# Two output projections emitted at block 13 instead of block 8 of the second chunk's FFN, their first loads tied to that block by one-column copies

## The chip, the cores and the metric

The kernel runs on one core of one Trainium2 chip. The metric is the device time of one execution in microseconds; the time before is the median of three runs, 3060.2 us. TensorE (PE), VectorE (DVE), ScalarE (ACT) and GpSimd (POOL) each work through their own instructions in the order in which the program lists them. SyncE (SP) and ScalarE also issue DMA transfers, each from its own list.

## What is computed

One layer of a decoder trunk on 2048 tokens of width 1024, in float32. The reference, cut to what matters here:

```
p = rms_norm(x, norm1_g) @ w_in
mix = concat(mlstm(p), rwkv7(p), diff_attention(p))      # 256 + 256 + 512 columns
x = x + mix @ w_out                                      # the output projection
h = rms_norm(x, norm2_g)
x = x + square(relu(h @ w_ff_up)) @ w_ff_down            # the FFN, width 4096
out = rms_norm(x, final_g)
```

Attention is causal, has 4 heads and works on blocks of 128 queries.

## The kernel before

The tokens are cut into four chunks of 512, numbered 0 to 3. After the input projection and the two recurrent groups, attention runs chunk after chunk and head after head (class `Attention`, lines 1004 to 1071). For a block of 128 queries it multiplies Q with K into PSUM tiles `pS` (lines 1026, 1027, 1029), moves them to the row `E` on DVE (L1030), takes exponentials on ACT (L1037), combines two rows on DVE (L1045), transposes `E` on PE into `pT` (L1051), copies it to `PT` on ACT (L1053) and multiplies it with V into `pO` (L1056). After four blocks of a head the result is normalised, transposed (L1068), copied to the tile `ot` (L1070) and stored to the scratch tensor `mixT` (L1071).

The tail (class `Tail`) does the output projection and the FFN. Every matrix product is done in three matmuls, on high and low parts of both operands (lines 182, 183, 184). Weights come in quarters of 128x512: a load into `wraw`, a split on ACT into `whi` (L174) and on POOL into `wlo` (L175). `Weights.get` has six pairs of `whi` and `wlo`, and three `wraw` tiles, or two where it is made with `raws=2`.

`ffn(x, h)` runs 16 blocks for one chunk. `up(fb)` multiplies two slices of `w_ff_up` with the hidden tiles `hh`, `hl` into two `pd` tiles and makes `ah`, `al` from them; `down(fb)` multiplies these with a slice of `w_ff_down` into eight `py` tiles, each added to `x` on DVE (L1175). The generator yields after `up(fb)` and before `down(fb - 1)`. A block is 48 + 48 matmuls of 128x512.

Chunk 0's and chunk 1's FFN are done in this way, beside the attention of chunks 2 and 3. The projections of chunks 2 and 3 (`outproj(2, ...)`, `outproj(3, ...)`) need all of the attention; the FFN of these two chunks is done together at the end by the class `Wino`, with seven products in place of eight. `Wino.first` and `Wino.second` normalise the projected chunks; their sums are PSUM tiles `nps` out of the same pool `pd` of two tiles that `up` uses, and they stand in the program behind each projection.

What sets the order: a scheduler gives every instruction a place by priority, which is the order of emission in the Python code (`high_priority` puts some ahead), among those whose operands and tiles it holds to be ready. Tiles of one pool and tag are handed out in the order of emission, so a block of the FFN that is emitted behind `Wino.second` gets its `pd` tiles behind those of `Wino.second`, and so behind both projections. The code around the change:

```
for fb in tl.ffn(x1, h1):                       # chunk 1
    if fb == 0:
        tl.final(0, x0, (2, 5))
    if fb == 8:
        actx.close()                            # attention's pools end here
        ...                                     # pq, tx2, th2, tw2: new pools in their memory
        w2 = Weights(..., "tw2", raws=2)
        raw2 = lambda: w2.wp.tile([P, T], F32, name="xr", tag="xr", bufs=3)
        outproj(2, tl.load(2, hp2, raw2), ...); wn.first(x2)
        outproj(3, tl.load(3, hp2, raw2), ...); wn.second(x2, x3, hp2)
```

`tl.load(c)` loads eight tiles `xr` from `mixT` and splits them into `hh` and `hl` of the pool `th2`. The new pools lie in memory that attention used, so the first loads into `xr` and `wraw` wait until attention is done with it.

Of the kernel before, what the change touches and what calls it, by code (L numbers as in the profile page):

```python
# [10 lines left out]
F32 = mybir.dt.float32  # L11
# [9 lines left out]
P = 128  # L21
# [4 lines left out]
T = 512  # L26
# [146 lines left out]
def split(nc, hi, lo, src, lo_eng):  # L173
    nc.scalar.activation(hi, src, AF.Copy)  # L174
    lo_eng.tensor_tensor(lo, src, hi.bitcast(F32), ALU.subtract)  # L175


def mm3(nc, out, pairs):

    n = len(pairs)  # L180
    for i, (sh, sl, mh, ml) in enumerate(pairs):
        nc.tensor.matmul(out, sh, mh, start=(i == 0), stop=False)  # L182
        nc.tensor.matmul(out, sh, ml, start=False, stop=False)  # L183
        nc.tensor.matmul(out, sl, mh, start=False, stop=(i == n - 1))  # L184
# [890 lines left out]
class Tail:  # L1075
# [73 lines left out]
    def ffn(s, x2, h2):  # L1149
        tc, nc = s.tc, s.tc.nc  # L1150
        FB = 16
        acts = {}

        def up(fb):
            w = s.w.get(s.wu[fb], 256)
            ah = s.ap.tile([P, 2, T], F32R, name="ah", tag="ah")
            al = s.ap.tile([P, 2, T], F32R, name="al", tag="al")
            for j in range(2):
                ps = s.pd.tile([P, T], F32, name="pd", tag="pd")
                mm3(nc, ps, [(*w(k, j * P, (j + 1) * P), h2[k][0], h2[k][1]) for k in range(KT)])  # L1160
                with tc.high_priority():
                    r = s.raw()
                    nc.scalar.activation(r, ps, AF.Relu)
                    nc.scalar.activation(r, r, AF.Square)
                    split(nc, ah[:, j], al[:, j], r, nc.vector)
            acts[fb] = (ah, al)

        def down(fb):
            w = s.w.get(s.wd[fb], 1024, kt=2)
            ah, al = acts.pop(fb)  # L1170
            for d in range(KT):
                ps = s.py.tile([P, T], F32, name="py", tag="py")
                mm3(nc, ps, [(*w(j, d * P, (d + 1) * P), ah[:, j], al[:, j]) for j in range(2)])
                with tc.high_priority():
                    nc.vector.tensor_tensor(x2[d], ps, x2[d], ALU.add)  # L1175

        up(0)
        yield 0
        for fb in range(1, FB):
            up(fb)  # L1180
            yield fb
            down(fb - 1)
        yield FB
        down(FB - 1)
# [299 lines left out]
def tile_hybrid_layer(ctx: ExitStack, tc: tile.TileContext, xt, wi, wg, wm, wo, wu, wd, vf, vg, lw, hb, tb, lq, cm, out, dbg=None, upto=9):  # L1484
    nc = tc.nc
# [98 lines left out]
    tl = Tail(ctx, tc, e, xt, wo, wu, wd, out)  # L1584
# [12 lines left out]
    for fb in tl.ffn(x1, h1):  # L1597
        if fb == 0:
            tl.final(0, x0, (2, 5))
        if fb == 8:  # L1600
            actx.close()
            with tc.using_default_side("right"):
                pq = [ctx.enter_context(tc.tile_pool(name=f"pq{i}", bufs=2, space=PSUM)) for i in range(2)]
                tl.xp2 = ctx.enter_context(tc.tile_pool(name="tx2", bufs=1))
                hp2 = ctx.enter_context(tc.tile_pool(name="th2", bufs=8))
                w2 = Weights(tc, e, rctx.enter_context(tc.tile_pool(name="tw2", bufs=1)), raws=2)
            raw2 = lambda: w2.wp.tile([P, T], F32, name="xr", tag="xr", bufs=3)
            for _ in tl.outproj(2, tl.load(2, hp2, raw2), x2, (0, 1), w2, raw2, pq[0], e.x2d[0]):
                pass
            wn = Wino(tl, pq)  # L1610
            wn.first(x2)
            for _ in tl.outproj(3, tl.load(3, hp2, raw2), x3, (4, 5), w2, raw2, pq[1], e.x2d[1]):
                pass
            wn.second(x2, x3, hp2)
# [76 lines left out]
```

## Time and profile before

| | us |
|---|---|
| median of 3 runs (3052.37 to 3060.57) | 3060.2 |
| the profiled execution | 3062.33 |
| span of the profiled execution | 3060.6 |
| PE busy in the span | 2907.0 (95%) |
| DVE / ACT / POOL busy | 1936.0 / 1295.7 / 1063.1 |
| mean granted TensorE clock, share of full speed | 0.963 |

The profiled execution lies 2.1 us above the median and 1.7 us above its own span. PE is busy nearly all the time, but a busy share says little by itself: matmuls are pipelined, and at half the granted clock the same matmul counts as busy for longer. So the stretches in which PE pauses, or in which the granted clock is under 1.00, are the ones to look at; start times of matmuls that follow each other tell what one costs.

### The profile page before, as it was taken

How to read it: one execution, taken by the hardware profiler on the slowest of the kernel's cores; microseconds unless marked ns; L12 is line 12 of the kernel's file. 1: busy time of each engine (PE TensorE's matmuls, PEld its weight loads, DVE VectorE, ACT ScalarE, POOL GpSimd, SP SyncE). 2: the span in 40 equal slices, each digit the busy share in tenths (PEclk: the TensorE clock that was granted, in tenths of full speed). 3: DMA queues.
4: the chain of work that ended last, by engine and by line, in shares of the span. 5: the costliest groups of instructions: out<-in, count | busy, mean ns of one | idle time of the engine just before them, and what ended most of it. 6: DMA issues, size and time to landing. Idle time of an engine off the chain costs nothing.

```text
span 3060.6 us, 47580 instructions
## 1 busy us (share of the span) xinstructions
PE 2907.0 (95%) x16880; PEld 2383.8 (78%) x16880; DVE 1936.0 (63%) x4358; ACT 1295.7 (42%) x2567; POOL 1063.1 (35%) x1016
## 2 busy tenths in 40 slices
PE   8999999999999889999999999997799899999998
PEld 7887887778878767888888788875677688888886
DVE  6587878678772456554555765562435766668788
ACT  5333334223322445544445544552234355554443
POOL 4353444333433214433333423422345322222232
PEclk9998999999999879999999989997899899999999
DMA  8445333643543553444446343334522244475441
GB/s 308 129 135 196 92 92 84 214 118 92 154 147 115 165 143 107 111 121 112 113 109 171 96 122 104 105 88 134 172 85 85 69 168 152 149 255 179 146 147 63
DMA packets 317096, 409.15 MB, mean 134 GB/s; under 512 B 102421, under 2 KB 164150, under 8 KB 315834
## 3 DMA queue, kind: packets, MB, share of 16 engines
q1 hardware_dynamic: 230154, 285.90, 30.7%
q10 hardware_dynamic: 86704, 120.21, 13.3%
q8 instruction: 133, 2.18, 0.3%
q14 instruction: 105, 0.86, 0.1%
HBM read 298.24 MB, written 107.76 MB: 133 GB/s over the span
## 4 chain that ended last, share of the span: by engine, by line
PE 56%; DVE 5%; DMA 4%; ACT 1%; issue 1%; POOL 1%; SPq 0%; ACTq 0%; DVEq 0%; POOLq 0%
PE pd L183 5%; PE pd L182 5%; PE pd L184 5%; PE pd L1224 5%; PE pd L1225 5%; PE pd L1226 5%; PE pO L1056 4%; PE py L182 4%; PE py L183 4%; PE py L184 3%; PE pS L1026 2%; PE pS L1027 2%; PE pT L1051 2%; PE py L1226 2%; PE py L1224 2%; PE py L1225 2%
## 5 line engine op out<-in xcount | busy, mean ns | idle before, releaser
L175 POOL TENSOR_TENSOR wlo<-wraw,whi 128x512 fp32r<-128x512 f32 (+2 forms) x432 | 595.4, 1391 | 849.7 <-ACT whi L174 611.3
L174 ACT ACTIVATE whi<-wraw 128x512 fp32r<-128x512 f32 (+2 forms) x432 | 267.4, 624 | 334.6 <-PE pd L183 103.3
L182 PE MATMUL pd<-hh,whi 128*128 128x512 f32 x768 | 304.0, 402 | 18.6 <-ACT whi L174 9.7
L175 POOL TENSOR_TENSOR wlo<-wr,whi 128x512 fp32r<-128x512 f32 x104 | 151.2, 1455 | 462.6 <-ACT whi L174 356.0
L183 PE MATMUL pd<-hl,whi 128*128 128x512 f32 x768 | 305.2, 398 | 1.0 <-DVE hl L175 1.0
L184 PE MATMUL pd<-hh,wlo 128*128 128x512 f32 x768 | 300.4, 397 | 1.4 <-POOL wlo L175 1.4
L1175 DVE TENSOR_TENSOR x<-py,x 128x512 f32<-128x512 f32 x256 | 174.9, 688 | 196.0 <-PE py L184 195.4
L1030 DVE TENSOR_SCALAR_CACHE_REDUCE E<-pS 128x512 f32<-128x512 f32 (+4 forms) x320 | 186.0, 607 | 146.1 <-PE pS L1027 85.6
L174 ACT ACTIVATE whi<-wr 128x512 fp32r<-128x512 f32 x224 | 140.4, 630 | 244.6 <-PE pd L1225 163.6
L182 PE MATMUL pd<-hhi,whi 128*128 128x512 f32 x544 | 224.2, 416 | 8.3 <-ACT hhi L279 7.4
L184 PE MATMUL pd<-hhi,wlo 128*128 128x512 f32 x544 | 224.4, 415 | 0.0
L183 PE MATMUL pd<-hlo,whi 128*128 128x512 f32 x544 | 223.2, 412 | 0.4 <-POOL hlo L175 0.3
L1224 PE MATMUL pd<-hh,whi 128*128 128x512 f32 x560 | 221.0, 396 | 1.5 <-DVE x L1348 1.3
L1226 PE MATMUL pd<-hh,wlo 128*128 128x512 f32 x560 | 221.5, 396 | 0.0
L1225 PE MATMUL pd<-hl,whi 128*128 128x512 f32 x560 | 221.5, 396 | 0.0
L182 PE MATMUL py<-ah,whi 128*128 128x512 f32 x512 | 206.3, 403 | 10.0 <-DVE x L1175 5.0
L183 PE MATMUL py<-al,whi 128*128 128x512 f32 x512 | 203.3, 397 | 0.6 <-DVE al L175 0.6
L184 PE MATMUL py<-ah,wlo 128*128 128x512 f32 x512 | 202.4, 397 | 0.0
L1037 ACT ACTIVATE E<-E,nm 128x128 f32<-128x128 f32 (+15 forms) x128 | 153.7, 1201 | 95.5 <-DVE nm L1033 81.0
L182 PE MATMUL pd<-whi,hhi 128*128 128x256 f32 (+1 forms) x640 | 188.0, 294 | 2.6 <-ACT gates L372 1.5
L183 PE MATMUL pd<-wlo,hhi 128*128 128x256 f32 (+1 forms) x640 | 187.9, 294 | 0.0
L182 PEld LDWEIGHTS pd<-hh,whi 128*128 128x128 f32 x768 | 146.5, 192 | 52.6 <-issue 11.2
(453 smaller groups left out, 7021.3 us busy)
## 6 DMA issues: line engine op xcount, KB each, us to landing
act<-x SPq DMA_DIRECT2D x96, 256.0 KB, 2.1
wraw<-in_wu ACTq DMA_DIRECT2D x64, 256.0 KB, 3.1
wraw<-in_wu SPq DMA_DIRECT2D x64, 256.0 KB, 3.2
wraw<-in_wd ACTq DMA_DIRECT2D x64, 256.0 KB, 3.2
wraw<-in_wd SPq DMA_DIRECT2D x64, 256.0 KB, 3.1
x<-act SPq DMA_DIRECT2D x56, 256.0 KB, 2.7
x<-act ACTq DMA_DIRECT2D x56, 256.0 KB, 4.9
wraw<-in_wi ACTq DMA_DIRECT2D x48, 256.0 KB, 3.5
```

What stands on the lines that cost most here:

```text
L174: nc.scalar.activation(hi, src, AF.Copy)
L175: lo_eng.tensor_tensor(lo, src, hi.bitcast(F32), ALU.subtract)
L182: nc.tensor.matmul(out, sh, mh, start=(i == 0), stop=False)
L183: nc.tensor.matmul(out, sh, ml, start=False, stop=False)
L184: nc.tensor.matmul(out, sl, mh, start=False, stop=(i == n - 1))
L1030: V.tensor_scalar(E[:, k0:k0 + w], s_[:, :w], 0.125, None, ALU.mult, ALU.max, accum_out=mb[:, j:j + 1])
L1037: A.activation(E[:, :n], E[:, :n], AF.Exp, bias=nm, accum_out=l)
L1056: PE.matmul(o[:, 0:P], pt[:, b * P:(b + 1) * P], vt[:, kb], start=(kb == 0), stop=(kb == i))
L1175: nc.vector.tensor_tensor(x2[d], ps, x2[d], ALU.add)
L1224: mm(ps, sh, mv[0], start=start, stop=False, skip_group_check=True)
L1225: mm(ps, sh, mv[1], start=False, stop=False, skip_group_check=True)
L1226: mm(ps, sl, mv[0], start=False, stop=True, skip_group_check=True)
```

## The change

The two projections are emitted when the FFN of chunk 1 yields block 13, no longer at block 8. `up` leaves its last `ah` tile in `s.mark`. Ahead of the projections five tiles are taken, the three `xr` and the two `wraw` of the new pools, and ACT copies one column of `ah` of block 13 into each of them. A load into one of these tiles then has to come behind its copy, and a copy behind `up(13)` and behind attention's last use of that memory.

```diff
@@ ffn, up(fb)
             acts[fb] = (ah, al)
+            s.mark = ah
@@ tile_hybrid_layer
     for fb in tl.ffn(x1, h1):
-        if fb == 8:
+        if fb == 13:
             actx.close()
...
             raw2 = lambda: w2.wp.tile([P, T], F32, name="xr", tag="xr", bufs=3)
+
+            with tc.high_priority():
+                for t in [raw2() for _ in range(3)] + [w2.wp.tile([P, T], F32, name="wraw", tag="wraw", bufs=2) for _ in range(2)]:
+                    nc.scalar.copy(t[:, 0:1], tl.mark[:, 0, 0:1].bitcast(F32))
             for _ in tl.outproj(2, tl.load(2, hp2, raw2), x2, (0, 1), w2, raw2, pq[0], e.x2d[0]):
```

What this makes of the order is shown at three places. The first is PE at the end of attention (tile numbers kept: `py_23306` and `py_23314` are `down(11)`, `pd_23378` is the second half of `up(13)`; `pd_22632` and `pd_22662` are the first tiles of projection 2). Before:

```order
L1051 MATMUL pT_17328<-ident_63,E_17243 128x128 x4
L1056 MATMUL pO_17294<-Vt_16952,PT_17333 128x128 x4
L1068 MATMUL pT_17352<-ident_63,osb_16955 128x128 x4
L182 MATMUL pd_22632<-hh_22560,whi_22607 128x512
L182 MATMUL pd_22662<-hh_22560,whi_22607 128x512
```

With the change:

```order
L182 MATMUL py_23306<-ah_22998,whi_23253 128x512
L1068 MATMUL pT_17352<-ident_63,osb_16955 128x128 x2
L183 MATMUL py_23306<-al_22999,whi_23253 128x512
L1068 MATMUL pT_17352<-ident_63,osb_16955 128x128 x2
L184 MATMUL py_23306<-ah_22998,wlo_23254 128x512
L183 MATMUL pd_23378<-hl_20970,whi_23329 128x512
L184 MATMUL pd_23378<-hh_20969,wlo_23330 128x512
L182 MATMUL pd_23378<-hh_20975,whi_23329 128x512
L182 MATMUL py_23314<-ah_22998,whi_23241 128x512
```

Before, attention's last steps stand one behind the other and the projection right behind them; with the change the matmuls of blocks 9 to 13 stand between the steps, and 47 more of the FFN stand between attention's last transposes and the projection's first matmul.

The second place is SP's list at the same point (`wraw` from `in_wu`, `in_wd` are FFN weights, from `in_wo` projection weights). Before:

```order
L1071 DMA mixT_305<-ot 128x512 x2
L42 DMA xr<-mixT_304 128x512
L42 DMA wraw<-in_wo 128x512
L42 DMA xr<-mixT_304 128x512 x2
L42 DMA wraw<-in_wo 128x512
```

With the change:

```order
L42 DMA wraw<-in_wu 128x512 x2
L42 DMA wraw<-in_wd 128x512 x2
L1071 DMA mixT_305<-ot 128x512
L42 DMA xr<-mixT_304 128x512 x2
L42 DMA wraw<-in_wu 128x512
L42 DMA wraw<-in_wo 128x512
L42 DMA wraw<-in_wu 128x512
L42 DMA xr<-mixT_304 128x512 x2
L42 DMA wraw<-in_wd 128x512
```

Sixteen loads of FFN weights now stand between the last two stores to `mixT`, and three loads of FFN weights stand among the projection's first loads behind the last store.

The third place is ACT's list at the same point. Before:

```order
L1070 COPY ot<-pT 128x512
L42 DMA wraw<-in_wo 128x512
L42 DMA xr<-mixT_304 128x512
L174 ACTIVATE hh<-xr 128x512
L174 ACTIVATE whi<-wraw 128x512
```

With the change:

```order
L1070 COPY ot<-pT 128x512
L174 ACTIVATE whi<-wraw 128x512 x2
L174 ACTIVATE ah<-traw 128x512
L174 ACTIVATE whi<-wraw 128x512
L1612 COPY xr<-ah 128x1 x3
L42 DMA wraw<-in_wu 128x512
L1612 COPY wraw<-ah 128x1 x2
L42 DMA xr<-mixT_304 128x512
L42 DMA wraw<-in_wo 128x512
L1163 ACTIVATE traw<-pd 128x512
L174 ACTIVATE whi<-wraw 128x512
```

The five copies stand behind the last `ot` copy and four splits, and the projection's loads behind the copies.

## Rows read from the trace of the kernel before

**Rows 1.** Busy time by stretch: us, each engine's busy us (instructions), granted clock, DMA.

```profile
core 0: us, PE busy (x) PEld busy (x) DVE busy (x) ACT busy (x) POOL busy (x), PEclk, DMA share, GB/s
1800.00:2000.00 200.00, 200.00 (x1049) 168.96 (x1048) 106.64 (x239) 97.14 (x162) 72.83 (x54) 1.00 0.40 109
...
2034.50:2089.10 54.60, 41.23 (x228) 32.95 (x226) 23.39 (x65) 20.42 (x36) 3.09 (x3) 0.80 0.05 15
2089.10:2151.80 62.70, 49.11 (x199) 37.65 (x198) 18.48 (x22) 21.69 (x36) 23.34 (x19) 0.91 0.59 187
2151.80:2222.90 71.10, 54.23 (x207) 42.18 (x208) 31.87 (x46) 17.82 (x30) 20.55 (x16) 0.84 0.52 165
2222.90:2361.60 138.70, 137.95 (x607) 113.82 (x605) 61.17 (x79) 55.93 (x95) 71.85 (x52) 1.00 0.31 92
```

**Rows 2.** PE's groups from 2034.5 to 2089.1: count | busy, mean ns | idle before, releaser.

```profile
L1056 PE MATMUL pO<-Vt,PT 128*128 128x128 f32 x116 | 21.5, 339 | 9.5 <-ACT PT L1053 9.5
L1051 PE MATMUL pT<-ident,E 128*128 128x128 f32 x58 | 11.1, 321 | 0.0
L1026 PE MATMUL pS<-Kst,Qd 128*128 128x512 f32 (+2 forms) x17 | 7.6, 447 | 0.7 <-DVE E L1030 0.7
L1027 PE MATMUL pS<-Kst,Qd 128*128 128x512 f32 (+2 forms) x18 | 6.9, 382 | 0.0
L1068 PE MATMUL pT<-ident,osb 128*128 128x128 f32 x8 | 1.8, 360 | 3.2 <-DVE osb L1065 3.2
```

**Rows 3.** PE in order of time: start, us, what, [idle before, releaser].

```profile
2046.49 1.16 PE L1056 MATMUL pO<-Vt,PT 128*128 128x128 f32 x8
2047.48 0.60 PE L1051 MATMUL pT<-ident,E 128*128 128x128 f32 x4
2047.84 0.47 PE L1026 MATMUL pS<-Kst,Qd 128*128 128x512 f32 x1
...
2071.67 2.08 PE L1056 MATMUL pO<-Vt,PT 128*128 128x128 f32 x8 [0.73 <-ACT PT L1053]
...
2087.96 1.17 PE L1068 MATMUL pT<-ident,osb 128*128 128x128 f32 x4 [3.24 <-DVE osb L1065]
2097.48 1.19 PE L182 MATMUL pd<-hh,whi 128*128 128x512 f32 x2 [8.34 <-ACT whi L174]
...
2220.90 2.07 PE L145 MATMUL nps<-traw,ones 128*128 128x512 f32 x2 [7.27 <-DVE traw L144]
```

**Rows 4.** Chain that ended last within 2000 to 2240: start, us, what.

```profile
2089.84 1.99 DMA mixT<-ot
2092.03 4.18 DMA xr<-mixT
...
2101.03 4.69 DMA wraw<-in_wo
2106.72 3.38 DMA wraw<-in_wo
2110.82 1.02 POOL wlo L175
...
2113.83 3.66 DMA wraw<-in_wo
```

**Rows 5.** ACT's instructions on few columns, whole span: count | busy, mean ns | idle before.

```profile
L372 ACT ACTIVATE gates<-pd,nsm 128x8 f32<-128x8 f32 x8 | 2.2, 270 | 0.0
L372 ACT ACTIVATE gates<-pd 128x8 f32<-128x8 f32 x8 | 1.4, 178 | 0.0
```

**Rows 6.** POOL's splits of FFN weights, 1800 to 2035: ns min/median/max.

```profile
L175 POOL TENSOR_TENSOR wlo<-wraw,whi x61: 1267/1296/3332, 1799.4 to 2034.0; 128x512 fp32r<-128x512 f32 x61
```

**Rows 7.** The page: ACT's split (count | busy, mean ns); DMA issues (median us to landing).

```profile
L174 ACT ACTIVATE whi<-wraw 128x512 fp32r<-128x512 f32 (+2 forms) x432 | 267.4, 624 | 334.6 <-PE pd L183 103.3
...
wraw<-in_wu ACTq DMA_DIRECT2D x64, 256.0 KB, 3.1
```

## The prediction, made before the changed kernel had run

> **What bounds the kernel now.** I first read busy time by stretch, because the mean over the span hides where PE pauses. From 1800 to 2000, with attention and the FFN mixed, PE is busy 200.00 of 200.00 us at granted clock 1.00; from 2222.9 to 2361.6, in the FFN alone, 137.95 of 138.70 [rows 1]. Between them lie three stretches in which it is not. From 2034.5 to 2089.1 attention finishes alone (41.23 busy of 54.60, clock 0.80); then come projection 2 (49.11 of 62.70, clock 0.91) and projection 3 with the norms (54.23 of 71.10, clock 0.84) [rows 1]. These 188.4 us are what the change touches.
>
> In the first stretch PE alternates `pO` and `pT` and waits 0.73 us for ACT's copy `PT` each time; all waits for `PT` make 9.5 us [rows 2, 3]. The granted clock sinks there: `pO` x8, which at full clock takes 2047.48 - 2046.49 = 0.99 us from start to start, is recorded with 2.08 instead of 1.16 us at 2071.67 [rows 3]. That is the 1.2 GHz level, after PE has paused for each copy.
>
> In the second and third stretch the chain that ended last is not PE's: store of `mixT` 1.99, load of `xr` 4.18, then loads of `wraw` from `in_wo` of 3.4 to 4.7 us with a split between them [rows 4]. With two `wraw` tiles a load waits until POOL has split the one before the last. So the projections go at the pace of their weights.
>
> **Work and loss, stretch by stretch.** A matmul of 128x512 costs 137.95 / 607 = 0.2273 us at full clock [rows 1]. Attention alone: 116 `pO` at 0.99 / 8 = 0.124 (14.4), 58 + 8 `pT` at 0.36 / 4 = 0.09 (5.9) [rows 2, 3], 35 `pS` at up to 0.2273 (7.9 at most, some are narrower), six FFN matmuls (1.4): 29.7 us. The stretch lasts 54.6, so **24.9 us** are lost to waits and the half clock. The projections hold 2 x 192 matmuls (87.3 us) and two norms (about 3 us), 90.3 in 133.8: **43.5 us** are lost. Behind them stand 606 matmuls of the FFN up to 2361.6, with nothing lost.
>
> **What the change moves.** The order shows where these 606 go: 404 (91.8 us) ahead of attention's last transposes, 47 (10.7) between these and the first matmul of projection 2, 30 (6.8) inside projection 2, and 125 (28.4) behind the norms of projection 3. Past that point the order of all engines is the old one but for line numbers.
>
> Step 1, attention's tail: 29.7 + 91.8 = 121.5 us of work. That leaves attention's own chain, which took 54.6 us alone, more than twice its time, so its copies should be hidden under FFN matmuls, as from 1800 to 2000, where the same mix lost nothing [rows 1]. I add 2 us for the last head, where there is less to mix; bounds 0 and 10 (the sum of the `PT` waits, if all stayed).
>
> Step 2, the projections. Their weight chain does not become faster; it starts at attention's end as before. So I keep the 133.8 us and ask what is added. The five copies are bounded by ACT's instructions on eight columns, 178 and 270 ns [rows 5]; I take 0.18, that of the form without a second operand, 0.9 in all. The Trainium skill, page "ScalarE: Activation LUTs", section "Rules for kernel authors", budgets about 0.3 us per activation and 0.83 ns per element. By that figure the copies would be an estimated 1.5 us, and the sum 0.6 us longer; the row speaks against it. Ahead of the copies stand four splits, 4 x 0.624 = 2.5 us [rows 7], which run beside the 1.99 us of the last store [rows 4]; they stick out by 0.5. A DMA issue of ACT between the copies brings the delay to **1.7 us**. Behind the copies on ACT wait the projection's loads, the relu of block 13's second half and the split for block 14; PE has the 47 matmuls (10.7 us) meanwhile, against 8.34 us of waiting before [rows 3].
>
> The eight FFN weights for `down(13)` and `up(14)`, which before had been split ahead of attention's end, are now split among those of the projection. Each takes POOL 1.30 us [rows 6]. If each stood in the way of a projection weight that were 10.4 us, if none 0. POOL is busy 23.34 of 62.70 us there [rows 1], so I take 37% of it, **3.9 us**; bounds 0 and 10.4. The 47 + 30 FFN matmuls fit into the 43.5 us that PE idles there.
>
> Step 3, behind the projections: 28.4 us of FFN, at full clock. The wait of 7.27 us for `nps` before it [rows 3] is part of the 133.8 and stays. What `Wino` does after it hides under blocks 14 and 15 as it hid under block 15 before, at the old order.
>
> **The sum.** Before, from 2034.5 to 2361.6: 327.1 us. After: 121.5 + 2 + 133.8 + 1.7 + 3.9 + 28.4 + 0.8 (what the FFN stretch lost, 138.70 - 137.95) = 292.1. The gain is **35.0 us**: 22.9 from attention's tail and 12 from FFN matmuls that fill pauses of the projections. Against the profiled execution of 3062.3 that is 3027.3; the median is 2.1 us lower, so I predict **3025 us** as a median.
>
> **Rivals.** *Attention paces PE.* In order as PE is, each `pO` that comes before its copy stops the FFN too. ACT now splits weights between the copies (0.624 each [rows 7]); two of these ahead of each of some 15 copies would cost 15 x 1.2 = 18 us and leave a gain of 17: 3043. Against it stands the stretch from 1800 to 2000 with the same mix. Chance 0.08.
>
> *POOL's splits stretch.* A split has taken up to 3332 ns where the median is 1296 [rows 6]. If ten splits of blocks 9 to 13 took 2.0 us more beside attention's work on DVE, and PE waited for each, that is 20 us: 3045. Most of the 61 lie near the median, so 0.03. The Trainium skill, "GPSIMD Engine Reference", section 1 (Specifications), says that GpSimd shares its SBUF interfaces with VectorE and contends with its instructions on two SBUF inputs, which speaks for this rival; the trace agrees no further than by that largest value.
>
> *The weights of blocks 9 to 13 starve* (the slower side). Their loads stand in the lists of SP and ACT among attention's loads, stores and copies. If each of the ten half blocks had to wait for one whole load and both splits, 3.1 + 0.62 + 1.30 = 5.0 us [rows 6, 7], that is 50 us: 15 slower than before, 3075. It decides from 35 / 10 = 3.5 us per half block. From 1800 to 2000 FFN and attention loads shared the same two lists and PE had no pause [rows 1]. Chance 0.06 for over 0.3% slower, this and all else of that sign.
>
> *Nothing is won.* If loads of FFN weights hold back those of the projection (8 x 3.1 us in the chain of loads [rows 7] = 25), they lose 25 - 12 = 13 us; if step 1 gives only 15, the time is some 3058. Chance 0.06. That the change does not do what it says, the FFN not moving ahead of attention's end, is excluded by the order except for how the times fall; it is counted here.
>
> **How the numbers follow.** The forecast, a gain of 18 to 44 us, has 0.77; attention pacing PE 0.08; POOL's splits 0.03; nothing won 0.06; slower 0.06. About 0.3%, 9 us, is what a measurement of this kernel can tell from no change; so faster is 0.88, the same 0.06, slower 0.06. With the bounds: at best 24.9 + 12 + 4 = 41 us are won, and runs of before lie up to 8 us under their median, so the low end is 3011. At worst within the forecast step 1 loses 10 and step 2 10.4, a gain of 20; with part of the pacing rival the high end is 3043.
>
> **What would show it.** In the changed kernel's profile: granted clock 1.00 and no `PT` waits above 0.3 us until attention's last `L1068`, which should come near 2158; the first projection matmul some 11 to 14 us later, with FFN matmuls between; `nps` of the second norm near 2290 to 2300, with its wait of about 7 us still there; then 28 us to the place that was at 2361.6 and is near 2327. I am wrong if PE shows waits for `whi` or `wlo` of FFN weights before attention's end, if the clock sinks there, or if the weight chain of the projections takes over 145 us.

## The result, and the profile after

The changed kernel takes 3017.0 us as the median of four runs (3012.9 to 3027.0) against 3060.4 for the kernel before (3052.4 to 3061.7): a ratio of 0.9879, interval 0.9858 to 0.9899, or 37 us less (31 to 43). The ratios here are those on record for the runs of one group; they differ a little from the quotient of the two medians, which would be 0.9858 here, or 43 us. The profiled execution took 3016.1 us with a span of 3014.2. Timed again in two more groups of runs, the ratio was 0.9888 (0.9863 to 0.9912) and 0.9889 (0.9862 to 0.9916), some 34 us. The prediction was 3025, a gain of 35.

To see where the time went I cut the profiles at four points that all kernels have in common: A, the transposes `L1068` of the head before attention's last two; T, attention's last `L1068`; N, the last sum of squares `nps` (L145) of the second norm; and B, the last L145 behind chunk 1's FFN (four more stand at the very end of the kernel). With the old order and with block 11 T is the first of the last four `L1068`, with FFN between them the third, 0.45 us later; so much the first two stages are uncertain against each other. The kernel before, A to T, T to N, N to B (columns as in [rows 1]):

```profile
1926.40:2087.96 161.56, 148.19 (x796) 123.80 (x795) 81.38 (x200) 73.86 (x125) 41.51 (x31) 0.93 0.29 80
2087.96:2220.90 132.94, 102.48 (x406) 79.57 (x406) 50.99 (x71) 39.51 (x66) 43.90 (x34) 0.87 0.56 176
2220.90:2424.90 204.00, 188.05 (x777) 151.28 (x778) 106.10 (x140) 82.25 (x142) 92.53 (x65) 0.94 0.23 66
```

The changed kernel, the same three stages:

```profile
1921.20:2150.50 229.30, 229.30 (x1200) 194.09 (x1199) 111.89 (x240) 107.04 (x182) 83.46 (x62) 1.00 0.33 92
2150.50:2288.60 138.10, 117.06 (x483) 90.84 (x481) 60.15 (x80) 47.20 (x85) 57.31 (x43) 0.94 0.59 187
2288.60:2378.80 90.20, 77.04 (x297) 59.05 (x298) 69.50 (x90) 40.80 (x72) 37.34 (x25) 0.90 0.11 33
```

The first stage holds 404 more matmuls (1200 against 796) and PE is busy in all of it, at clock 1.00. The second holds 77 more and is only 5.2 us longer. The third is shorter by what has left it. From A to B it is 457.6 us in place of 498.5. What comes behind B is the same within 0.4 us (3014.2 - 2378.8 = 635.4 against 3060.6 - 2424.9 = 635.7). A itself comes 5.2 us earlier, in a part that the change doesn't touch, so that is no gain of the change.

PE's groups from 2034.5 to 2150.9 in the changed kernel answer to [rows 2]:

```profile
L1056 PE MATMUL pO<-Vt,PT 128*128 128x128 f32 x116 | 15.5, 275 | 0.0
L1051 PE MATMUL pT<-ident,E 128*128 128x128 f32 x58 | 8.9, 272 | 0.0
L1068 PE MATMUL pT<-ident,osb 128*128 128x128 f32 x8 | 1.5, 271 | 0.0
```

The 9.5 us that PE waited for `PT` and the 3.2 us for `osb` are 0.0. These matmuls are also recorded shorter, `pO` with 275 ns against 339.

PE in order of time in the changed kernel, the rows that answer to [rows 3]: attention's end, the first matmul of projection 2 and what it still waits for, the waits of the norms, and the place that stood at 2361 before.

```profile
2150.54 0.38 PE L1068 MATMUL pT<-ident,osb 128*128 128x128 f32 x2
...
2162.56 0.39 PE L182 MATMUL pd<-hh,whi 128*128 128x512 f32 x1
...
2164.00 0.50 PE L184 MATMUL pd<-hh,wlo 128*128 128x512 f32 x1 [0.35 <-POOL wlo L175]
...
2253.51 0.47 PE L182 MATMUL pd<-hh,whi 128*128 128x512 f32 x1 [2.21 <-ACT nacc L155]
...
2280.31 1.02 PE L162 MATMUL nps<-ones,nacc 128*128 128x1 f32 x8 [3.18 <-DVE nacc L159]
...
2288.61 2.08 PE L145 MATMUL nps<-traw,ones 128*128 128x512 f32 x2 [7.28 <-DVE traw L144]
...
2320.07 0.39 PE L182 MATMUL py<-ah,whi 128*128 128x512 f32 x1
```

The wait of 8.34 us ahead of the projection is gone: 47 FFN matmuls stand there. The norms' waits of 2.21, 3.18 and 7.28 us are still there, as before (2.29, 3.18, 7.27).

### The profile page after: what moved, and what is told of

The parts are those of the page before. It is cut to its first block, busy times and chain, and to the rows that moved or that the text cites. A ratio compares the mean times of both kernels' runs of the same rounds, so it can differ in the third digit from the quotient of the medians.

```text
span 3014.2 us, 47526 instructions
## 1 busy us (share of the span) xinstructions
PE 2879.8 (96%) x16880; PEld 2362.2 (78%) x16880; DVE 1938.6 (64%) x4358; ACT 1293.8 (43%) x2572; POOL 1062.7 (35%) x1016
## 3 DMA queue, kind: packets, MB, share of 16 engines
q10 hardware_dynamic: 86704, 120.21, 13.5%
## 4 chain that ended last, share of the span: by engine, by line
PE 56%; DMA 5%; DVE 4%; ACT 1%; issue 1%; POOL 1%; SPq 1%; ACTq 0%; DVEq 0%; POOLq 0%
PE pd L182 5%; PE pd L183 5%; PE pd L184 5%; PE pd L1227 5%; PE pd L1226 5%; PE pd L1225 5%; PE pO L1056 4%; PE py L182 3%; PE py L183 3%; PE py L184 3%; PE pS L1026 2%; PE pS L1027 2%; PE py L1225 2%; PE py L1227 2%; PE py L1226 2%; PE pT L1051 2%
## 5 line engine op out<-in xcount | busy, mean ns | idle before, releaser
L1037 ACT ACTIVATE E<-E,nm 128x128 f32<-128x128 f32 (+15 forms) x128 | 153.7, 1201 | 90.7 <-DVE nm L1033 74.9
L184 PE MATMUL pd<-whi,hlo 128*128 128x256 f32 (+1 forms) x640 | 187.3, 293 | 0.0
```

The lines of the kernel that those rows point to most:

```text
L1037: A.activation(E[:, :n], E[:, :n], AF.Exp, bias=nm, accum_out=l)
```

## Experiments

Landmark A to B, with its three stages, for all kernels that have a profile, in us. The rows come in groups of 2, 4, 4 and 4 that ran together, each of the last three on one chip (the second and the fourth on the same); a ratio is to runs of the kernel before in the same group, whose median was 3060.4, 3046.5, 3046.8 and 3058.1 us. So times of different groups do not compare directly; their ratios do.

| kernel | A to T | T to N | N to B | A to B | time, ratio to before |
|---|---|---|---|---|---|
| before | 161.6 | 132.9 | 204.0 | 498.5 | 3060.4 |
| changed | 229.3 | 138.1 | 90.2 | 457.6 | 3017.0, 0.9879 |
| e1_nocopy | 229.3 | 133.5 | 90.7 | 453.5 | 3008.2, 0.9857 |
| e2_copy8 | 155.3 | 132.2 | 203.0 | 490.5 | 3050.1, 1.0006 |
| e3_at11 | 207.5 | 129.3 | 138.1 | 474.9 | 3033.1, 0.9943 |
| e3_at14 | 229.3 | 163.0 | 76.6 | 468.9 | 3023.7, 0.9913 |
| e0_before | 155.2 | 130.9 | 201.8 | 487.9 | 3045.2 (one run) |
| e0_after | 229.3 | 135.9 | 91.9 | 457.1 | 3013.9, 0.9888 |
| e4_raws3 | 229.3 | 130.4 | 90.7 | 450.4 | 3008.9, 0.9864 |
| e4_raws1 | 229.3 | 194.2 | 92.1 | 515.6 | 3068.1, 1.0065 |
| e5_after2 | 229.3 | 140.6 | 91.8 | 461.7 | 3020.4, 0.9889 |
| e5_nocopy2 | 229.3 | 132.7 | 91.6 | 453.6 | 3014.6, 0.9880 |
| e5_nocopy_raws3 | 229.5 | 126.0 | 90.9 | 446.4 | 3012.5, 0.9867 |
| e4_bufs5 | 229.3 | 135.1 | 89.6 | 454.0 | 3017.5, 0.9888 |

### Copies or place? One part alone

The change has two parts. The first run keeps the new place and leaves the copies out:

```diff
         if fb == 13:
...
-            with tc.high_priority():
-                for t in [raw2() for _ in range(3)] + [...]:
-                    nc.scalar.copy(t[:, 0:1], tl.mark[:, 0, 0:1].bitcast(F32))
```

> The change without the five copies: the projections are emitted at block 13 and nothing else. My theory (the place of emission lets blocks 9 to 13 run beside attention's tail, the copies only hold the first loads back and cost about 1.7 us) gives the time of the changed kernel, 3017 us, within 5; FFN matmuls between attention's last transposes and the first projection matmul fall from 47 to 36 by the order. Rival (the copies are what keeps the projection's loads out of the way of the FFN's weights in SP's and ACT's lists): FFN weights are late, PE waits for whi in attention's tail, and the time is between 3035 and 3060.

Measured: 3008.2 us (3004.2 to 3012.7) against 3046.5 for the kernel before on that chip, ratio 0.9857 (0.9813 to 0.9902). All of the gain is there without the copies. (In time it is 9 us under the 3017 of the first group where 5 were allowed, but the kernel before is 14 us lower in this group too; the forecast number of 36 matmuls ahead of the projection is what the trace has.) The second run has the copies at the old place:

```diff
         if fb == 8:
...
+            with tc.high_priority():
+                for t in [raw2() for _ in range(3)] + [...]:
+                    nc.scalar.copy(t[:, 0:1], tl.mark[:, 0, 0:1].bitcast(F32))
```

> The copies alone: they read ah of block 8, and the projections are emitted at block 8 as in the kernel before. My theory: attention's tail is as lonely as before, so 3060 us, plus 1 to 2 for the copies. Rival (the copies bring the gain): near 3017.

Measured: 3050.1 us, ratio 1.0006 (0.9979 to 1.0033). The copies alone bring nothing. So the cause of the gain is the place of emission. That it acts through the FFN's `pd` tiles, which no longer stand behind those of the projections, is read from the code; emission also sets the priority, and no run separates the two.

### Where along the FFN? Block 11 and block 14

The change with `fb == 11` and with `fb == 14` in place of `fb == 13`:

```diff
-        if fb == 13:
+        if fb == 11:      # e3_at11;  fb == 14: e3_at14
```

> The change at block 11 in place of 13. By the order 267 FFN matmuls (60.7 us) then stand among attention's tail, none between its end and the projections, none among the projections. My theory splits the gain in two: cover of attention's tail (23 us; 60.7 us of FFN are more than the 25 us that the tail lost, so most of it is won) and FFN that fills pauses of the projections (12 us; all of it gone here, with the 8 us wait for the first loads back). So 3060 - 23 + 2 = about 3038, range 3032 to 3045. Rival (all of the gain is the tail's cover): 3020. Rival (attention paces PE, and only the whole of 381 matmuls covers it): 3050.

Measured: 3033.1 us, ratio 0.9943 (0.9923 to 0.9964), a gain of about 17 us. The three stages of its profile:

```profile
1914.40:2121.90 207.50, 203.59 (x1085) 172.56 (x1083) 103.93 (x230) 98.76 (x167) 75.51 (x55) 1.00 0.32 93
2121.90:2251.20 129.30, 101.48 (x407) 77.96 (x407) 51.53 (x71) 39.96 (x71) 43.98 (x34) 0.89 0.56 181
2251.20:2389.30 138.10, 123.05 (x490) 97.29 (x491) 84.24 (x111) 57.22 (x100) 59.96 (x41) 0.91 0.18 52
```

Two blocks fewer are enough for most of attention's tail (PE idles 3.9 us in it), but none is left for the projections: their stage has the 407 matmuls and the 129.3 us that it has in the kernel before. So the gain is nearly that of the tail alone. It is smaller than the 22 us that I had expected, though the time lies in my range, because the kernel before is faster in this group. Against the old order in the same group (e2_copy8, 155.3 us from A to T at full clock) 289 more matmuls, 65.7 us of work, cost 52.2 us: 13.5 are won, not 23. I had counted 267 matmuls.

> The change at block 14. By the order the 381 FFN matmuls among attention's tail are the same, 156 in place of 47 stand between its end and the first projection matmul, some 20 in place of 30 among the first projection, one block less behind. My theory (the projections go at the pace of their weight loads, whose chain starts only when ah of block 14 is there; the FFN ahead of it does not fill its later pauses): 3017 within 8, since the wait for the first loads is hidden in both. Rival (any FFN block put ahead of the projections fills pauses of them): 2995 to 3005. Rival (Wino's preparation loses its cover of two blocks behind the projections): 3025 to 3035.

Measured: 3023.7 us, ratio 0.9913 (0.9884 to 0.9943), a gain of about 26 us. By its profile it is slower than the change, 468.9 us from A to B against 457.1 to 461.7 in three profiles of the change. But the intervals of the two ratios overlap, and the profiled execution, 3030.6 us, was the slowest of seven (the fastest took 3009.9), so that block 14 is slower than block 13 is not shown by time. Its last two stages:

```profile
2154.60:2317.60 163.00, 139.41 (x579) 109.07 (x577) 67.36 (x90) 55.55 (x99) 67.43 (x51) 0.95 0.54 171
2317.60:2394.20 76.60, 56.86 (x204) 42.57 (x205) 62.32 (x81) 32.12 (x58) 26.24 (x17) 0.85 0.04 11
```

PE's waits for the additions to `x` in the last stage (in all, times, longest), here and in the changed kernel:

```profile
PE py L182 <- DVE x L1176: 13.1, 4, 8.6
...
PE py L182 <- DVE x L1176: 2.1, 3, 1.2
```

The first load of a projection weight in this run, where T is at 2154.61:

```profile
2184.49 0.44 ACTq L42 DMA_DIRECT2D wraw<-in_wo  x1
```

The extra block puts 96 more matmuls (21.8 us at 0.2273) into the projection stage, which becomes 24.9 us longer than the changed kernel's 138.1: on balance they fill nothing. The trace shows why: the copies tie the loads to `ah` of block 14 and run only from 2183.8 to 2184.2, so the first projection weight is issued 29.9 us after T, and 4.7 in the changed kernel. That is 25.2 later, about the whole difference. Behind the projections 93 fewer are left, 21.1 us, but the stage is shorter by only 13.6. DVE is busy 62.32 of 76.60 us there, and PE waits for its additions to `x` 13.1 us, where it waits 2.1 in the changed kernel. In this profile too little FFN is left to stand beside DVE's work, which is near what the second rival had named. As a number the time is within 8 of my 3017, but as a gain, 26 us (17 to 35), it lies where that rival had put it, 25 to 35 below 3060; so the time leaves the two open. The block to choose seems to have two sides, enough ahead to fill the projections and enough behind to cover DVE, but block 14 without the copies, which would not hold the loads back, was not run.

### The same two programs profiled once more

The difference from A to B in the first pair of profiles, 40.9 us, is more than my steps explain. The kernel before and the changed one were therefore profiled a second time, without any edit.

> The kernel before once more, only to see how much two profiles of the same program differ, stage by stage. Landmarks that all kernels share: attention's L1068 of the third head before the end (1926.4 in the first profile) and the last sum of squares L145 of the product stage (2424.9). Between them the first profile took 498.5 us, the changed kernel 457.6: 40.9 less, of which my steps explain 35. If the other 6 us are variation between executions, this profile has under 495 us between the landmarks; if they are the change's, it has 497 to 500. The projection stage, from attention's last L1068 to the last sum of the second norm, should be 131 to 134 us in both cases.

> The changed kernel once more, timed and profiled on the chip of the three runs beside it. Time ratio 0.985 to 0.990 of the kernel before (first result 0.988). Between the two landmarks (L1068 of the third last head, last L145) 455 to 461 us if the stage repeats, and no wait of TensorE from the first landmark to attention's end. It is the base for the runs with one and three load tiles.

Measured: 487.9 and 457.1 us from A to B, a difference of 30.8; in time 3013.9 for the changed kernel, ratio 0.9888. The changed kernel repeats within 0.5 us (a third profile, below, has 461.7). The kernel before does not: it takes 10.6 us less, 6.4 of them from A to T. The first stage of this second profile of the kernel before:

```profile
1919.70:2074.94 155.24, 141.69 (x796) 118.26 (x795) 81.35 (x200) 73.59 (x124) 41.44 (x31) 1.00 0.30 84
```

Its last part, attention alone, which took 54.60 us at clock 0.80 in [rows 1]:

```profile
2027.80:2074.90 47.10, 33.59 (x224) 26.68 (x222) 22.68 (x63) 20.29 (x36) 3.08 (x3) 1.00 0.06 18
```

And PE in order of time there (the row at 2071.67 of [rows 3] took 2.08 us with the same wait):

```profile
2065.90 1.16 PE L1056 MATMUL pO<-Vt,PT 128*128 128x128 f32 x8 [0.73 <-ACT PT L1053]
2066.89 0.60 PE L1051 MATMUL pT<-ident,E 128*128 128x128 f32 x4
```

The same matmuls with the same 0.73 us waits ran at full clock here, and 7.5 us less were lost. The run with copies at block 8 shows it too (155.3 us from A to T). So these pauses did not always bring the granted clock to the 1.2 GHz level. The three profiles of this stage with the old order are each from another group of runs, so they can't tell chip from execution. The timed runs speak for the execution: 21 runs of the kernel before on one chip took 3040.1 to 3066.7 us, and on the whole the slower ones had the lower mean granted clock (0.971 for the fastest, 0.964 for the slowest). In which stage these lost it, the times do not say.

### Do the projections go at the pace of their weights?

The changed kernel with one `wraw` tile for the projections, and with three (with five pairs of `whi` and `wlo` for room), in place of two; the copies' list is adapted:

```diff
-                w2 = Weights(..., raws=2)
+                w2 = Weights(..., raws=1)              # e4_raws1
+                w2 = Weights(..., bufs=5, raws=3)      # e4_raws3
```

> The changed kernel with one wraw tile for the projections in place of two (one copy ties it). If the chain of load and splits sets the pace, each of the 32 quarters now takes a whole load of some 3.7 us, a split on ACT beside one on POOL of 1.3 and the issue of the next, about 5.6 us: 179 us from attention's end to the second norm's last sum in place of 138, so some 35 to 45 us slower than the changed kernel, about where the kernel before is (3040 to 3055). If TensorE or the norms set the pace of this stage, it costs under 10 us.

> The changed kernel with three wraw tiles for the projections in place of two (and five pairs of whi and wlo in place of six, to fit the memory; a third copy ties the third tile). My theory, that the projections go at the pace of their weights because a load waits for the split of the quarter two before, says that the stage from attention's end to the second norm's last sum falls from 138 us; but of its some 21 us of TensorE's idle time 12.7 are the norms' own chain (2.21, 3.18 and 7.28 us), which stays, so that 3 to 8 us are to be won and the ratio is 0.983 to 0.987. Rival: the transfers themselves are the limit (the DMA engines are 58% busy there), or five pairs are too few: then it is within 2 us of the changed kernel or slower.

Measured: with one tile 3068.1 us, ratio 1.0065 (1.0037 to 1.0093); the stage T to N takes 194.2 us in place of 135.9, 58 more, where I had expected 35 to 45 (the time is 54 above the changed kernel's). My 179 us for the stage had left out the norms' waits of 3.2 and 7.1 us, which the chain does not cover; with them it is 189. PE's longest waits in that stage, with one tile (in all, times, longest):

```profile
PE pd L182 <- ACT whi L174: 34.6, 25, 3.4
PE pd L184 <- POOL wlo L175: 5.8, 24, 0.7
```

With three tiles 3008.9 us, ratio 0.9864 (0.9834 to 0.9893) against 0.9888 beside it; the stage takes 130.4 us, 5.5 less, as the theory said; the intervals of the times overlap. PE waits for `whi` no more (1.1 us with two tiles), and a new wait has come. That wait, and what DVE did ahead of it:

```profile
PE pd L182 <- DVE x L1127: 6.2, 1, 6.2
...
2228.65 7.10 DVE L1233 SCALAR_TENSOR_TENSOR x<-x,vf,nacc 128x512 f32<-128x512 f32 x8 [0.30 <-ACT nacc L168]
```

The loads themselves show the pace. The last of the 32 projection weights is issued 175.3, 109.9 and 100.6 us after T with one, two and three tiles, so one load follows the other every 5.5, 3.4 and 3.1 us. With one tile the chain of load and split sets the pace, and with two it still sets the end of the loads. A third tile brings that end 9.3 us forward, but the stage only 5.5: now the eight multiplications of the first norm on DVE (L1233, 7.10 us) stand ahead of a projection's addition (L1127), and PE waits 6.2 us for it.

### Control, and the parts together

Five pairs alone (two `wraw` tiles), the change and the change without copies once more, and no copies with three tiles, on one chip:

```diff
-                w2 = Weights(..., raws=2)
+                w2 = Weights(..., bufs=5, raws=2)      # e4_bufs5
+                w2 = Weights(..., bufs=5, raws=3)      # e5_nocopy_raws3, the three lines of the copies left out
```

> The changed kernel again, as the base for the three runs beside it on their chip: ratio 0.986 to 0.990. Stage times as before: 229.3 us from the third last head's L1068 to attention's end, 135 to 139 to the second norm's last sum, 90 to 92 to the last L145.

> The changed kernel with five pairs of whi and wlo in place of six and still two wraw tiles: the control for the run with three. If the third wraw tile made the gain of that run (projection stage 130.4 in place of 135.9), this one is within 2 us of the changed kernel; if fewer pairs made it by another order, this one gains as much.

> The change without the copies, beside the changed kernel on one chip. The profiles differ by 2 to 5 us in the projection stage only (133.6 without copies, 138.1 and 135.9 with them). If the copies delay the projection's first loads, which is what my 1.7 us stood for, it is 2 to 5 us faster than the changed kernel; if the earlier difference was variation between executions, it is within 2 us of it.

> Without copies and with three wraw tiles (five pairs of whi and wlo): if the two act on different waits, the projection stage takes 126 to 130 us and the kernel is 6 to 10 us faster than the changed one, ratio 0.982 to 0.986. If both only shorten the same fixed idle time of the norms' chain, it is no faster than the better of the two, 4 to 5 us.

Measured: 3020.4, 3017.5, 3014.6 and 3012.5 us, ratios 0.9889 (0.9862 to 0.9916), 0.9888 (0.9858 to 0.9919), 0.9880 (0.9851 to 0.9910) and 0.9867 (0.9837 to 0.9897). The change alone took 140.6 us from T to N, above the 135 to 139 that I had written. Five pairs hardly explain the gain of three tiles: their ratio is that of the changed kernel, their stage takes 135.1 us, 4.7 more than with three tiles, and the last load is issued 110.1 us after T (109.9 to 113.3 with six pairs). But beside the changed kernel of their own group (140.6) their stage is 5.5 us shorter, as much as the third tile gave in the other group. As the changed kernel's stage differs by 4.7 us between its own profiles, one profile of each does not make this control sharp.

The projection stage of no copies and three tiles:

```profile
2156.90:2282.89 125.99, 112.37 (x483) 88.80 (x481) 60.80 (x80) 45.94 (x80) 58.72 (x43) 0.97 0.64 205
```

With 126.0 us it is the shortest of all, and the two savings roughly add in the profile: its last load is issued 96.9 us after T. By time this version is 7.9 us below the changed kernel on the same chip, under the 9 us that a measurement of this kernel can tell, and the intervals overlap: that it beats the changed kernel is likely, not shown. The same holds for no copies alone, 5.9 us below it, where I had expected 2 to 5 if the copies delay the loads.

What the copies cost is seen in ACT's list. In the changed kernel (the third and last rows are DMA issues):

```profile
2154.60 0.36 ACT L1612 COPY xr<-ah 128x1 f32<-128x1 f32 x3
2154.86 0.18 ACT L1612 COPY wraw<-ah 128x1 f32<-128x1 f32 x1
2154.89 0.34 ACTq L42 DMA_DIRECT2D xr<-mixT  x1
2154.96 0.18 ACT L1612 COPY wraw<-ah 128x1 f32<-128x1 f32 x1
2155.27 0.44 ACTq L42 DMA_DIRECT2D wraw<-in_wo  x1
```

Without the copies (e1_nocopy), where T is at 2151.15:

```profile
2154.27 0.35 ACTq L42 DMA_DIRECT2D wraw<-in_wo  x1
2154.68 0.62 ACT L174 ACTIVATE whi<-wraw 128x512 fp32r<-128x512 f32 x1
2154.98 0.36 ACTq L42 DMA_DIRECT2D wraw<-in_wu  x1
```

ACT's first load of a projection weight is issued 4.73 us after T with the copies and 3.12 without, and with them a load of an FFN weight goes first. In the stage T to N the difference is 5.1 us (138.1, 135.9 and 140.6 with copies, mean 138.2; 133.5 and 132.7 without, mean 133.1). With three profiles against two, the single differences run from 2.4 to 7.9 us. The loads show how 1.6 us grow. ACT's second load of a projection weight in the changed kernel and in e1_nocopy:

```profile
2164.44 0.34 ACTq L42 DMA_DIRECT2D wraw<-in_wo  x1
...
2161.41 0.45 ACTq L42 DMA_DIRECT2D wraw<-in_wo  x1
```

This is 13.9 us after T against 10.3, 3.6 later, and the last of the 32 is issued 111.0 us after T against 107.5. PE's idle time in the stage is some 3 us longer in the mean (21.2 against 18.1); the other 2 us are matmuls recorded longer. With the copies at block 8 (e2_copy8), where no FFN weight stands among the first of these loads, the stage is 132.2 us, between the 132.9 and 130.9 without them. So it does not seem to be the five instructions themselves that cost.

## Why the prediction was right, and which of its steps were not

The time (3025 against 3017.0) lies in the range, and the gain of 35 us beside 37, 34 and 34 measured (43 by the medians of the first group). By its steps:

**The loss in attention's tail.** The prediction counted 24.9 us as lost and 22.9 as won (its four terms make 29.6 of work, not 29.7, which changes nothing). In the first pair of profiles, 404 FFN matmuls (91.8 us) cost 229.3 - 161.6 = 67.7 us, so 24.1 were won; in the second pair 74.1, so 17.7. The step was right on the mechanism and on the profile that it was read from. But some 7 us of the loss were the half clock of that one execution, which the second profile of the same program did not have: by the prediction's own working it gives 47.1 - 29.7 = 17.4 us. The prediction's sentence that the clock sinks "after PE has paused for each copy" is true of that trace and was no rule. The waits, 9.5 for `PT` and 3.2 for `osb`, were there in both.

**Nothing lost in the mix.** 121.5 us of work plus 2 for the last head were predicted from 2034.5 on. Measured with A's earlier start taken out: 229.3 - (2034.5 - 1926.4) = 121.2. The 2 us were not needed, and attention did not pace PE: `pO` waits 0.0 us. T is at 2150.54; with the 5.2 us by which A is earlier it would be 2155.7, where "near 2158" had been said.

**The projections.** 139.4 us were forecast as 133.8 + 1.7 + 3.9, and the stage takes 138.1, or 5.2 longer than before, and 5.0 longer in the second pair. The sum was right and the two terms in it, by these profiles, were not. The copies were sized at 1.7 us and cost about 5.1 in the mean (2.4 to 7.9), as the runs without them show; the POOL splits with all else were sized at 3.9, and without copies the stage is 133.1 against 131.9 before (mean of 132.9 and 130.9), 1.2 us. The errors cancelled; that the sum came out is luck. The copies themselves take 0.18 us each, as [rows 5] had said:

```profile
L1612 ACT COPY xr<-ah x3: 173/185/186, 2154.6 to 2154.8; 128x1 f32<-128x1 f32 x3
```

The 0.3 us per activation that the Trainium skill budgets (page "ScalarE: Activation LUTs", section "Rules for kernel authors") is, in that row of the page, for one whose bias is a pointer operand, which a copy does not have; the prediction left that condition out. What was missed is not the copies' duration but the place of the loads behind them.

**The pace of the weights.** That the projections go at the pace of load and split was read from the chain that ended last [rows 4]. It is still so in the changed kernel:

```profile
2174.83 3.58 DMA wraw<-in_wo
2178.43 0.64 ACT whi L174
2179.14 1.27 POOL wlo L175
...
2182.42 3.22 DMA wraw<-in_wo
```

The runs with one and three tiles bear it out, 58 us more and 5.5 less, though not for the whole stage: behind the last load another 27 us pass, with the last quarters and the second norm. The filling of the pauses was predicted at 12 us; it is 17.5 for 77 matmuls less 5.2 and 5.0, so 12.3 and 12.5.

**Behind the projections.** The 481 matmuls that left (109.3 us) shortened the stage by 113.8 and 109.9 us. The first is 4.5 more than forecast and the second 0.6, so most of the surplus lies in the execution and is not the change's. With it the parts make up, as they must, the differences from A to B: 24.1 + 12.3 + 4.5 = 40.9 in the first pair, and 17.7 + 12.5 + 0.6 = 30.8 in the second; the prediction had 22.9 + 12 + 0.1. The place that was at 2361 comes at 2320.07, with A's 5.2 us taken out at 2325.3, and "near 2327" had been said.

**The rivals.** No wait for `whi` or `wlo` stands in the first stage, where PE is busy 229.30 of 229.30 us, so the weights of blocks 9 to 13 did not starve. POOL's splits kept their median. In the changed kernel from 1921.4 to 2146.1:

```profile
L175 POOL TENSOR_TENSOR wlo<-wraw,whi x60: 1267/1294/3077, 1921.4 to 2146.1; 128x512 fp32r<-128x512 f32 x60
```

The largest, 3077 ns, is no larger than the 3332 of [rows 6], and PE did not wait for it.

## What to carry to other kernels

Work that needs the same pool of PSUM tiles as a long chain of loads should be emitted ahead of that chain, as much of it as fills the pauses of what runs beside it, and no more than leaves the next stage its cover: block 11 left the projections unfilled, block 14, in its one profile, left DVE uncovered. Where a tie of loads is added to keep an order, look whether the order holds without it; here the place of emission alone made the gain, and the ties cost some microseconds in the profile. A tie also sets when the chain of loads starts: at block 14 it held the first load back by 25 us. When a stage's loss is read from one profile, split it into waits and half clock: the waits came back in all three profiles with the old order, the half clock did not.

## What the runs showed that was not expected

The granted clock of the same matmuls with the same pauses was 0.80 in one profile of the kernel before and 1.00 in another, 54.60 against 47.10 us. And the profiles without copies suggest that five instructions of 0.18 us each, put ahead of a queue's loads, can lengthen a stage of 133 us by some 5, not by their own time, for at block 8 they cost nothing that the profiles show, but by the order and the start of the loads behind them.
